# Two fused transformer blocks: both norms behind the first MLP from one inverse root, queries and keys left raw, the residual scaled when it is loaded

## The chip, the cores and the metric

The kernel runs on one core of one Trainium2 chip. The metric is the device time of one execution in microseconds (us). Engines are named as in the profile: PE is TensorE, PEld its weight loads, DVE is VectorE, ACT is ScalarE, POOL is GpSimd, SP is the SyncE queue, which here issues DMAs.

## What is computed

Two blocks run one after the other on x of 1 x 1024 x 1024 (tokens x channels). The change sits between them:

```python
# end of the first block
x = x + squared_relu_mlp(rmsnorm(x, norm_ffn), ffn_w1, ffn_w2)
x = rmsnorm(x, norm_final)            # x * rsqrt(mean(x*x) + 1e-6) * g
# start of the second block
h = rms_norm(x, norm1_g)
z = h @ w_in                          # pool, sconv, conf and attention columns
...
q = rms_norm(q, q_norm_g); k = rms_norm(k, k_norm_g)   # over 32 channels of a head half
mix = concat([y_pool, y_sconv, y_conf, y_attn])
x = x + mix @ w_out                   # residual: the normed x
h2 = rms_norm(x, norm2_g)
x = x + (silu(h2 @ w_gate) * (h2 @ w_up)) @ w_down
```

So two norms follow each other directly (norm_final, then norm1_g), and the normed x is needed twice: as input of w_in and as the residual that w_out's product is added to.

## The kernel before

**Layout.** Activations lie with channels on the 128 partitions: x is eight tiles x_k of 128 channels x 1024 tokens, 512 KB each, which live in a ring of 40 slots (`self.u`). Each matmul is done three times in split precision (high and low parts, names ending in h and l, such as hh, hl, yh, yl, wh, wl). A GEMM of one output tile is two halves of 512 tokens, each 8 x 3 matmuls into one PSUM bank, which DVE (or ACT) then evacuates.

**Order.** Generators are the tasks; `drive` (L262) runs the task with the best priority whose operands are there by the kernel's own clock model (class `Clock`, L86). The order in which the instructions come out is the order on each engine, and each engine's queue runs in order. So a different number or kind of instructions moves all that follows them.

**Norms (L1764).** When the last MLP tile is added up, DVE has two sums of squares per token: `acc` of x, `acf` of x times the gain of norm_final. `first_norms` turns them (`tokensum`, PE transposes named cs), takes the inverse root rf of the first mean (`rsqrt`, L790: 11 small dependent DVE instructions on tiles ry, rq, rp), from rf and acf the mean of the second norm, a second inverse root r1, and the product r1f. PE spreads it over partitions (`tok_bcast`, PE matmuls tb, ACT copies) as r1b, the row factor of the second block; then rf is spread as rfb.

**Residual (L1786).** `final_out` makes the residual: for each x_k ACT multiplies by the gain, POOL by rfb (tensor_tensor 128x1024), SP stores it to DRAM (xd2). At w_out (L1936) each tile is loaded again as x4 and the GEMM's halves are added to it.

**Queries and keys (L2073).** `zt` evacuates a GEMM of w_in and multiplies by r1b on DVE; only the first one (RZ = 1) is copied raw by ACT and multiplied later. `attn_qk` squares (ACT, zsq), turns (PE, zn), sums 32 channels (DVE, zv), takes an inverse root of 128x32, spreads it (PE, zb), scales, splits, and stores to DRAM (qkd), from where the attention loads it stacked (stk). Beside this POOL computes the low part wl of every weight tile.

**The rest of the second block.** In ORDER2 (L72): attention heads 0 and 1, conf (a 31-tap convolution, some 46 DVE instructions per tile), sconv, conf, sconv, attention heads 2 and 3, pool, pool. The mixed outputs y are split (yh, yl) for w_out; PE's pp matmuls are the pool's, waiting for DVE's pld.

Of the kernel before, what the change touches and what calls it, by code (L numbers as in the profile page):

```python
# [11 lines left out]
AF = mybir.ActivationFunctionType  # L12
ALU = mybir.AluOpType
# [3 lines left out]
D = 1024  # L17
# [3 lines left out]
EPS = 1e-6  # L21
# [41 lines left out]
CL = 2.5  # L63

NP = (1, 2, 3, 4, 5)

RZ = 1

W2 = 6

# [158 lines left out]
class Kern:  # L229
# [1531 lines left out]
        self.psd = self.psx.enter_context(self.tc.tile_pool(name="psd", bufs=2, space=bass.MemoryType.PSUM))  # L1761


    def first_norms(self, xs):  # L1764


        nc, gv = self.nc, self.gv
        yield [self.acc, self.acf]
        pf = yield from self.tokensum(self.acf, "vf")
        rf = yield from self.rms_col(self.acc, D)  # L1770
        v2 = self.small("v2", 8)
        nc.vector.tensor_tensor(v2, rf, rf, ALU.mult)
        nc.vector.tensor_tensor(v2, v2, pf[:, :8], ALU.mult)
        nc.vector.tensor_scalar(v2, v2, 1.0 / D, EPS, ALU.mult, ALU.add)
        r1 = yield from self.rsqrt(v2, 8)
        r1f = self.small("r1f", 8)
        nc.vector.tensor_tensor(r1f, r1, rf, ALU.mult)
        self.rb2 = self.u("r1b")
        yield from self.tok_bcast(r1f, self.rb2)
        self.ev_rb2.set(self.rb2)  # L1780
        rfb = self.u("rfb")
        yield from self.tok_bcast(rf, rfb)
        self.acc = self.acf = None
        self.spawn(self.final_out(xs, rfb), 4)

    def final_out(self, xs, rfb):  # L1786
        nc = self.nc
        for k in range(8):
            yield [rfb]
            nc.scalar.activation(xs[k], xs[k], AF.Copy, scale=self.gv[:, G_FIN + k:G_FIN + k + 1])  # L1790
            nc.gpsimd.tensor_tensor(xs[k], xs[k], rfb, ALU.mult)
            yield [xs[k]]
            nc.sync.dma_start(self.xd2[k], xs[k])
            xs[k] = None

    def bias_tiles(self):

# [47 lines left out]
    def second(self, xs, out):  # L1845

        nc = self.nc
# [13 lines left out]
        def zt(p, into=None, raw=False):  # L1861
            t = self.u(p)

            def evac(sl, ps):
                if raw:
                    nc.scalar.activation(t[:, sl], ps, AF.Copy)
                else:
                    nc.vector.tensor_tensor(t[:, sl], ps, (into or self.rb2)[:, sl], ALU.mult)
            yield from self.big(hs, evac, () if raw else extra)
            return t  # L1870
# [15 lines left out]

        self.ydirect = [k for k in self.yorder if len(ORDER2) - ND <= at[k] < len(ORDER2) and k < 4]
        self.ys, self.ev_ys, self.heads = {}, evs(6), 0
        for n, (name, j) in enumerate(ORDER2):
            if n == NL:  # L1890
                for k in self.yorder:
                    if k not in self.ydirect:
                        self.spawn(self.load_split(self.yd[k], "y", self.ys, k, self.ev_ys[k], [self.ev_y[k]]), 5)
            if name == "attn":
                for a in range(2):
                    raw = 2 * j + a < RZ
                    t = yield from zt("zqk", raw=raw)
                    self.spawn(self.attn_qk(j, a, t, raw), 1)
                t = yield from zt("zv")
                self.spawn(self.attn_v(j, t), 1)  # L1900
                for hh in range(2):
                    self.spawn(self.attention(2 * j + hh), 2)
                del t
            elif name == "conf":
                a = yield from zt("ca")
                g_ = yield from zt("cg")
                self.spawn(self.conf_in(j, a, g_), 3)
                del a, g_
            elif name == "sconv":
                c = yield from zt("sc")  # L1910
                sh = yield from zt("sh", c)
                b = yield from zt("sb")
                self.spawn(self.sconv(j, sh, b), 3)
                del c, sh, b
            else:
                z = yield from zt("zp")
                self.spawn(self.poolmix(j, z), 3)
                del z
        self.h2 = hs = None

        xs = []
        ys, ev, ev6 = self.ys, self.ev_ys, Event()
        def part(ps, w, h, n, k):
            sl = slice(h * 512, h * 512 + 512)
# [5 lines left out]
        def added(x, ps, h):  # L1930
            sl = slice(h * 512, h * 512 + 512)
            with self.tc.high_priority(PRI):
                nc.vector.tensor_tensor(x[:, sl], ps, x[:, sl], ALU.add)

        first = self.pairs_begin(38, True)
        for mt in range(8):  # L1936
            if mt > 4:
                next(first)
            if mt == 1 and ahead:
                self.wnext()  # L1940
                xs.append(x2)
                continue
            x = self.u("x4")
            nc.sync.dma_start(x, self.xd2[mt])
            xs.append(x)
            w = self.wnext()
            ahead = mt == 0 and self.heads == 4
            if ahead:

                w2 = self.wready[self.wat]  # L1950
                x2 = self.u("x4")
                nc.sync.dma_start(x2, self.xd2[1])
                d = self.s2("gm")
                ps = [self.b("gm"), self.b("gm"), d[:, 0:512], d[:, 512:1024]]
                for n, k in enumerate(self.yorder):
                    yield [ev[k]]
                    for q in range(4):
                        part(ps[q], w2 if q > 1 else w, q % 2, n, k)
                for q in range(4):
                    added(x2 if q > 1 else x, ps[q], q % 2)  # L1960
                del d, ps, w2
                continue
            for h in range(2):
                ps = self.b("gm")
                for n, k in enumerate(self.yorder):
                    yield [ev[k]]
                    part(ps, w, h, n, k)
                added(x, ps, h)
        ys.clear()
        self.spawn(self.load_split(self.yd[6], "y", ys, 6, ev6, [self.ev_y[6]]), 5)  # L1970
        yield [ev6, self.ev_o]
# [33 lines left out]
        for q in range(11):  # L2005
# [36 lines left out]
            t = self.u("ft")  # L2042
# [27 lines left out]
        for hh in range(2):  # L2070
            self.ev_vT[2 * j + hh].set(v)

    def attn_qk(self, j, a, t, raw):  # L2073
        nc, gv, cst = self.nc, self.gv, self.cst
        if raw:

            yield [t, self.ev_rb2]
            nc.vector.tensor_tensor(t, t, self.rb2, ALU.mult)
            yield [t]
        sq = self.u("zsq")  # L2080
        nc.scalar.activation(sq, t, AF.Square)
        yield [sq, self.free_s()]
        v = self.small("zv2", 32)
        for half in range(2):
            yield [self.free_s()]
            pt = self.transpose4(sq, half, "zn")
            nc.vector.tensor_reduce(v[:, half * 16:half * 16 + 16], pt.rearrange("p (c d) -> p c d", d=32), AX.X, ALU.add)

        if a == 0:
            nc.vector.tensor_scalar(v, v, 32 * EPS, None, ALU.add)  # L2090
        else:
            nc.vector.tensor_scalar(v, v, 1.0 / 32, EPS, ALU.mult, ALU.add)
        rs = yield from self.rsqrt(v, 32)
        gcol = G_QG if a == 0 else G_KG
        for hf in range(2):
            ps = yield from self.bcast4(rs[:, hf * 16:hf * 16 + 16], "zb", 4)
            sl = slice(hf * 512, hf * 512 + 512)
            nc.vector.scalar_tensor_tensor(t[:, sl], t[:, sl], gv[:, gcol:gcol + 1], ps, ALU.mult, ALU.mult)
        for x, half in enumerate(self.split_new(t, "zqk")):
            yield [half]  # L2100
            nc.sync.dma_start(self.qkd[j, a, x], half.bitcast(F32))
        self.nqk[j] += 1
        if self.nqk[j] == 2:
            self.ev_qk[j].set()
# [234 lines left out]
    def main(self):  # L2339
        self.plan()  # L2340
        xs = yield from self.mixer()
        nrm = yield from self.cross(xs)
        self.h2 = []
        self.xd2 = self.dram("xd2", [8, 128, 1024])
        self.ev_rb2 = Event()
        nc, gv = self.nc, self.gv
        gg = self.small("gg", 8, tag="gg", bufs=1)
        nc.vector.tensor_tensor(gg, gv[:, G_FIN:G_FIN + 8], gv[:, G_N1:G_N1 + 8], ALU.mult)

        def done(k, xs):  # L2350
            if k == 0:
                self.acc, self.acf = self.u("acc"), self.u("acf")
            self.h2.append(self.split_new(xs[k], "h", gg[:, k:k + 1]))
            self.sumsq(self.acc, xs[k], k == 0)
            self.sumsq(self.acf, xs[k], k == 0, gv[:, G_FIN + k:G_FIN + k + 1])
            if k == 7:
                self.spawn(self.first_norms(xs), 0)
        self.bias, self.ev_b = [[] for _ in range(4)], [Event() for _ in range(4)]
        yield from self.mlp(nrm, done)
        del nrm  # L2360
        yield from self.second(None, self.o["out"])
# [110 lines left out]
```

## Time and profile before

| | us |
|---|---|
| median of 3 runs (2617.35 to 2618.97) | 2618.58 |
| the profiled execution | 2613.1 |
| its span | 2611.2 |
| PE busy in it | 2499.2 |
| DVE busy | 1563.7 |
| ACT busy | 855.6 |
| POOL busy | 820.5 |

PE is busy for 96% of the span, so a gain has to come from PE's idle time or from PE's clock: the mean granted clock is 0.983 of full speed. Times in the rows are us from the span's start. A bracket in a row is the idle time of that engine before the instruction and what ended it.

### The profile page before, as it was taken

To read this page: it belongs to the slowest core of one execution; us is meant where nothing else is said; L and a number is where in the kernel's file an instruction comes from. 1 tells how busy PE (TensorE), PEld (TensorE's weight loads), DVE (VectorE), ACT (ScalarE), POOL (GpSimd) and SP (SyncE) were. 2 spreads that over 40 slices of the span, in tenths; PEclk is the share of its full clock that TensorE was granted. 3 is DMA by queue.
4 is the path that set the end of the run, shared out by engine and by line. 5 is a ranking of instruction groups with operands and counts; after the bars stand their busy time and mean duration, and the time that the engine had idled before them with its cause. 6 is when DMAs were issued, how large, how long until landed. Compare 5 with 4: busy or idle time off the path is not lost.

```text
span 2611.2 us, 30369 instructions
## 1 busy us (share of the span) xinstructions
PE 2499.2 (96%) x11880; PEld 2057.4 (79%) x11880; DVE 1563.7 (60%) x2316; ACT 855.6 (33%) x1220; POOL 820.5 (31%) x349
## 2 busy tenths in 40 slices
PE   8999999999989999999999798988989999999999
PEld 6788877888877888778888587776867888887887
DVE  7873767554457665553434857976676665664433
ACT  6422343333343333321213423434452222222210
POOL 1122121211244454322222421121245656662221
PEclk9999999999999999999999898999989999999999
DMA  3223156421132333542211232143222222236212
GB/s 130 77 77 94 63 173 207 171 89 49 65 129 82 120 105 121 227 145 99 98 57 49 97 105 57 41 145 93 85 81 73 81 89 89 65 128 235 81 49 89
DMA packets 99134, 268.25 MB, mean 103 GB/s; under 512 B 19976, under 2 KB 34480, under 8 KB 98992
## 3 DMA queue, kind: packets, MB, share of 16 engines
q1 hardware_dynamic: 78400, 192.40, 21.5%
q10 hardware_dynamic: 20592, 73.93, 8.5%
q8 instruction: 93, 1.52, 0.2%
q14 instruction: 49, 0.40, 0.1%
HBM read 196.55 MB, written 69.74 MB: 102 GB/s over the span
## 4 chain that ended last, share of the span: by engine, by line
PE 81%; DVE 11%; DMA 3%; issue 2%; ACT 2%; POOL 1%; SPq 0%; ACTq 0%; POOLq 0%; DVEq 0%
PE gm L210 46%; PE q L210 26%; DVE cy L210 1%; PE apo L210 1%; PE xs L210 1%; PE as L210 1%; PE xo L210 1%; DVE rq L210 1%; DVE ry L210 1%; DMA stk<-qkd 1%; POOL wl L210 1%; PE pk L210 1%; PE pb L210 1%; PE apt L210 1%; DVE sb L210 1%
## 5 line engine op out<-in xcount | busy, mean ns | idle before, releaser
L210 POOL TENSOR_TENSOR wl<-wr,wh 128x1024 fp32r<-128x1024 f32 (+1 forms) x137 | 339.7, 2481 | 1354.0 <-ACT wh L210 1302.2
L210 DVE TENSOR_TENSOR x<-gm,x 128x512 f32<-128x512 f32 x304 | 208.9, 688 | 346.2 <-PE gm L210 345.5
L210 ACT ACTIVATE wh<-wr 128x1024 fp32r<-128x1024 f32 (+2 forms) x147 | 153.2, 1042 | 621.7 <-PE gm L210 589.5
L210 PE MATMUL gm<-fhh,wh 128*128 128x512 f32 x864 | 337.6, 391 | 5.3 <-ACT fhh L210 4.6
L210 PE MATMUL gm<-fhl,wh 128*128 128x512 f32 x864 | 336.9, 390 | 1.0 <-DVE fhl L210 1.0
L210 PE MATMUL gm<-fhh,wl 128*128 128x512 f32 x864 | 336.6, 390 | 0.0
L210 PE MATMUL gm<-hh,wh 128*128 128x512 f32 x800 | 324.6, 406 | 11.5 <-ACT hh L210 7.3
L210 PE MATMUL gm<-hl,wh 128*128 128x512 f32 x800 | 318.3, 398 | 0.5 <-DVE hl L210 0.5
L210 PE MATMUL gm<-hh,wl 128*128 128x512 f32 x800 | 316.7, 396 | 0.0
L210 PEld LDWEIGHTS gm<-fhh,wh 128*128 128x128 f32 x864 | 162.2, 188 | 42.7 <-ACT fhh L210 5.4
L210 PEld LDWEIGHTS gm<-fhl,wh 128*128 128x128 f32 x864 | 162.3, 188 | 35.3 <-DVE fhl L210 2.2
L210 PEld LDWEIGHTS gm<-fhh,wl 128*128 128x128 f32 x864 | 162.3, 188 | 33.9
L210 PEld LDWEIGHTS gm<-hh,wh 128*128 128x128 f32 x800 | 152.9, 191 | 43.1 <-ACT hh L210 8.3
L210 PEld LDWEIGHTS gm<-hh,wl 128*128 128x128 f32 x800 | 152.7, 191 | 32.4 <-issue 0.5
L210 PEld LDWEIGHTS gm<-hl,wh 128*128 128x128 f32 x800 | 153.2, 191 | 31.4 <-DVE hl L210 1.9
L210 POOL TENSOR_TENSOR wl<-pr,wh 128x1024 fp32r<-128x1024 f32 x37 | 88.7, 2398 | 118.7 <-ACT wh L210 118.7
L210 POOL TENSOR_TENSOR wl<-sa,wh 128x1024 fp32r<-128x1024 f32 x37 | 89.1, 2409 | 107.3 <-ACT wh L210 104.3
L210 POOL TENSOR_TENSOR pl<-sb,ph 128x1024 fp32r<-128x1024 f32 x38 | 92.0, 2421 | 81.0 <-ACT ph L210 81.0
L210 PE MATMUL q<-th,wh 128*128 128x512 f32 x296 | 116.8, 395 | 0.0
L210 PE MATMUL q<-th,wl 128*128 128x512 f32 x296 | 116.3, 393 | 0.0
L210 PE MATMUL q<-tl,wh 128*128 128x512 f32 x296 | 116.2, 392 | 0.0
L210 PE MATMUL q<-th,p 128*128 128x512 f32 x304 | 103.5, 402 | 3.2 <-DVE pc L210 3.2
(461 smaller groups left out, 5233.6 us busy)
## 6 DMA issues: line engine op xcount, KB each, us to landing
fhr<-hd SPq DMA_DIRECT2D x54, 512.0 KB, 5.0
wr<-in_w_in_dram ACTq DMA_DIRECT2D x39, 512.0 KB, 3.5
xd<-x SPq DMA_DIRECT2D x32, 512.0 KB, 2.6
x<-xd SPq DMA_DIRECT2D x32, 512.0 KB, 5.4
pr<-in_ffn_w_dram SPq DMA_DIRECT2D x32, 512.0 KB, 3.6
wr<-in_ffn_w_dram ACTq DMA_DIRECT2D x32, 512.0 KB, 3.5
hd<-ft SPq DMA_DIRECT2D x27, 512.0 KB, 5.0
hd<-pc SPq DMA_DIRECT2D x27, 512.0 KB, 5.7
```

The source lines that it names most:

```text
L210: ins = f(*args, **kw)
```

## The change

The two means become v and v2 = 1e-6 v + mean(acf), and r1f is the one inverse root of v2; v's own root rf is taken after it and only kept as a small tile. All four query and key GEMMs are now copied raw by ACT, and the factor's place in their norm is a term 32e-6 times v2 added to the sum of squares. The unscaled x_k are stored as soon as they are there; rfb is spread only before the last of ORDER2's tiles; each residual tile is loaded by a task of its own and scaled by DVE (scalar_tensor_tensor 128x1024: times gain, times rfb).

```diff
@@ -63,8 +63,6 @@
-RZ = 1
...
@@ -1761,37 +1759,42 @@
-    def first_norms(self, xs):
+    def first_norms(self):
...
         yield [self.acc, self.acf]
+        v = yield from self.tokensum(self.acc, "v")
         pf = yield from self.tokensum(self.acf, "vf")
-        rf = yield from self.rms_col(self.acc, D)
-        v2 = self.small("v2", 8)
-        nc.vector.tensor_tensor(v2, rf, rf, ALU.mult)
-        nc.vector.tensor_tensor(v2, v2, pf[:, :8], ALU.mult)
-        nc.vector.tensor_scalar(v2, v2, 1.0 / D, EPS, ALU.mult, ALU.add)
-        r1 = yield from self.rsqrt(v2, 8)
-        r1f = self.small("r1f", 8)
-        nc.vector.tensor_tensor(r1f, r1, rf, ALU.mult)
+        self.rf = self.small("rf", 8, tag="rf", bufs=1)
+        self.v2 = self.small("v2", 8, tag="vrow", bufs=1)
+        nc.vector.tensor_scalar(v, v, 1.0 / D, EPS, ALU.mult, ALU.add)
+        nc.vector.tensor_scalar(pf, pf, 1.0 / D, None, ALU.mult)
+        nc.vector.scalar_tensor_tensor(self.v2, v, EPS, pf, ALU.mult, ALU.add)
+        self.ev_v2.set(self.v2)
+        r1f = yield from self.rsqrt(self.v2, 8)
         self.rb2 = self.u("r1b")
...
         self.ev_rb2.set(self.rb2)
-        rfb = self.u("rfb")
-        yield from self.tok_bcast(rf, rfb)
+        rf = yield from self.rsqrt(v, 8)
+        nc.vector.tensor_copy(self.rf, rf)
         self.acc = self.acf = None
-        self.spawn(self.final_out(xs, rfb), 4)
-    def final_out(self, xs, rfb):
-        nc = self.nc
-        for k in range(8):
-            yield [rfb]
-            nc.scalar.activation(xs[k], xs[k], AF.Copy, scale=self.gv[:, G_FIN + k:G_FIN + k + 1])
-            nc.gpsimd.tensor_tensor(xs[k], xs[k], rfb, ALU.mult)
-            yield [xs[k]]
-            nc.sync.dma_start(self.xd2[k], xs[k])
-            xs[k] = None
+    def residual(self, k, ev):
+        x = self.u("x4")
+        self.nc.sync.dma_start(x, self.xd2[k])
+        yield [x, self.ev_rfb]
+        self.nc.vector.scalar_tensor_tensor(x, x, self.gv[:, G_FIN + k:G_FIN + k + 1], self.rfb, ALU.mult, ALU.mult)
+        self.x4[k] = x
+        ev.set(x)
+    def final_row(self):
+        self.rfb = self.u("rfb")
+        yield from self.tok_bcast(self.rf, self.rfb)
+        self.ev_rfb.set(self.rfb)
     def bias_tiles(self):
@@ -1886,16 +1889,18 @@
         self.ys, self.ev_ys, self.heads = {}, evs(6), 0
+        self.ev_rfb, self.x4, ev4 = Event(), [None] * 8, evs(8)
         for n, (name, j) in enumerate(ORDER2):
+            if n == len(ORDER2) - 1:
+                self.spawn(self.final_row(), 4)
             if n == NL:
...
                 for a in range(2):
-                    raw = 2 * j + a < RZ
-                    t = yield from zt("zqk", raw=raw)
-                    self.spawn(self.attn_qk(j, a, t, raw), 1)
+                    t = yield from zt("zqk", raw=True)
+                    self.spawn(self.attn_qk(j, a, t), 1)
                 t = yield from zt("zv")
...
@@ -1918,7 +1923,9 @@
-        xs = []
+        xs = self.x4
+        for mt in range(2):
+            self.spawn(self.residual(mt, ev4[mt]), 4)
         ys, ev, ev6 = self.ys, self.ev_ys, Event()
         def part(ps, w, h, n, k):
...
@@ -1938,26 +1945,24 @@
                 self.wnext()
-                xs.append(x2)
+                self.spawn(self.residual(mt + 2, ev4[mt + 2]), 4)
                 continue
-            x = self.u("x4")
-            nc.sync.dma_start(x, self.xd2[mt])
-            xs.append(x)
+            if mt + 2 < 8:
+                self.spawn(self.residual(mt + 2, ev4[mt + 2]), 4)
             w = self.wnext()
...
                 w2 = self.wready[self.wat]
-                x2 = self.u("x4")
-                nc.sync.dma_start(x2, self.xd2[1])
                 d = self.s2("gm")
...
                         part(ps[q], w2 if q > 1 else w, q % 2, n, k)
+                yield ev4[:2]
                 for q in range(4):
-                    added(x2 if q > 1 else x, ps[q], q % 2)
+                    added(xs[q // 2], ps[q], q % 2)
                 del d, ps, w2
...
@@ -1965,7 +1970,12 @@
                     part(ps, w, h, n, k)
-                added(x, ps, h)
+                yield [ev4[mt]]
+                added(xs[mt], ps, h)
+        for e in ev4:
+            e.aps = []
+        self.rfb = self.x4 = None
+        self.ev_rfb.aps = []
         ys.clear()
...
@@ -2070,13 +2080,10 @@
-    def attn_qk(self, j, a, t, raw):
+    def attn_qk(self, j, a, t):
         nc, gv, cst = self.nc, self.gv, self.cst
-        if raw:
-            yield [t, self.ev_rb2]
-            nc.vector.tensor_tensor(t, t, self.rb2, ALU.mult)
-            yield [t]
+        yield [t]
         sq = self.u("zsq")
...
@@ -2085,11 +2092,12 @@
-        if a == 0:
-            nc.vector.tensor_scalar(v, v, 32 * EPS, None, ALU.add)
-        else:
-            nc.vector.tensor_scalar(v, v, 1.0 / 32, EPS, ALU.mult, ALU.add)
+        yield [v, self.ev_v2]
+        w = v.rearrange("p (t g) -> p t g", g=4)
+        nc.vector.scalar_tensor_tensor(w, self.v2.unsqueeze(2).broadcast_to([128, 8, 4]), 32 * EPS, w, ALU.mult, ALU.add)
+        if a:
+            nc.vector.tensor_scalar(v, v, 1.0 / 32, None, ALU.mult)
         rs = yield from self.rsqrt(v, 32)
...
@@ -2342,7 +2350,7 @@
         self.xd2 = self.dram("xd2", [8, 128, 1024])
-        self.ev_rb2 = Event()
+        self.ev_rb2, self.ev_v2 = Event(), Event()
         nc, gv = self.nc, self.gv
...
@@ -2353,8 +2361,10 @@
             self.sumsq(self.acf, xs[k], k == 0, gv[:, G_FIN + k:G_FIN + k + 1])
+            self.spawn(self.store(self.xd2[k], xs[k]), 2)
+            xs[k] = None
             if k == 7:
-                self.spawn(self.first_norms(xs), 0)
+                self.spawn(self.first_norms(), 0)
         self.bias, self.ev_b = [[] for _ in range(4)], [Event() for _ in range(4)]
...
```

Three places of the new order. First ACT at the start of the second block, before and then in the change (zqk: raw query or key, zsq: its square, zbr: the inverse root on its way to PE, rfb: the spread rf, x: residual tiles):

```order
L210 ACTIVATE rfb_10858<-tb_10859 128x512
L210 ACTIVATE rfb_10858<-tb_10865 128x512
L210 ACTIVATE zsq_10875<-zqk_10708 128x1024
L210 ACTIVATE x_8342<-x_8342,gv 128x1024
L210 ACTIVATE x_8344<-x_8344,gv 128x1024
L210 ACTIVATE x_8346<-x_8346,gv 128x1024
L210 ACTIVATE x_8350<-x_8350,gv 128x1024
L210 ACTIVATE wh_10947<-wr_10822 128x1024
L210 ACTIVATE zsq_10955<-zqk_10817 128x1024
```

```order
L208 ACTIVATE zqk_10715<-gm_10749 128x512
L208 ACTIVATE r1b_10813<-tb_10814 128x512
L208 ACTIVATE r1b_10813<-tb_10820 128x512
L208 ACTIVATE zsq_10862<-zqk_10715 128x1024
L208 DMA wr_10963<-in_w_in_dram 128x1024
L208 ACTIVATE zqk_10848<-gm_10855 128x512
L208 ACTIVATE zbr_10921<-ry_10893 128x512
L208 ACTIVATE zbr_10932<-ry_10893 128x512
L208 ACTIVATE zqkh_10940<-zqk_10715 128x1024
L208 ACTIVATE wh_10959<-wr_10853 128x1024
L208 ACTIVATE zqk_10848<-gm_10902 128x512
L208 ACTIVATE zsq_10973<-zqk_10848 128x1024
```

The four x rows are gone here (eight in all), and both halves of the second zqk are evacuated on ACT, ahead of its zsq.

Then DVE at the end of the pools (pld: the pool's last step, yl: low part of a mixed output, amx, ars, ap: attention heads 2), before and in the change:

```order
L210 SCALAR_TENSOR_TENSOR pld_13024<-pl_13020,cst,zp_12924 128x1008
L210 TENSOR_TENSOR pld_13024<-pl_13020,zp_12924 128x16
L210 RECIPROCAL ars_13062<-asm_12852 128x2
L210 TENSOR_SCALAR ars_13062<-asm_12852,nlam_10700,ars_13062 128x1
L210 SCALAR_TENSOR_TENSOR ap_13013<-ap_13013,ars_13062 128x128
L210 RECIPROCAL ars_13063<-asm_13048 128x2
L210 TENSOR_REDUCE amx_13060<-as_13135 128x2
L210 TENSOR_TENSOR yl_13065<-yr_12915,yh_13064 128x1024
L210 TENSOR_TENSOR yl_13069<-py_13031,yh_13068 128x1024
L210 TENSOR_SCALAR ars_13063<-asm_13048,nlam_10700,ars_13063 128x1
L210 TENSOR_REDUCE amx_13146<-as_13148 128x2
L210 TENSOR_TENSOR yl_13081<-yr_12950,yh_13080 128x1024
```

```order
L208 SCALAR_TENSOR_TENSOR pld_13013<-pl_13009,cst,zp_12892 128x1008
L208 TENSOR_TENSOR pld_13013<-pl_13009,zp_12892 128x16
L208 TENSOR_REDUCE amx_13039<-as_13041 128x2
L208 SCALAR_TENSOR_TENSOR x_2349_13017<-x_2349_13017,gv,rfb_12917 128x1024
L208 TENSOR_TENSOR yl_13027<-py_12988,yh_13026 128x1024
L208 SCALAR_TENSOR_TENSOR x_2350_13019<-x_2350_13019,gv,rfb_12917 128x1024
L208 RECIPROCAL ars_13054<-asm_12816 128x2
L208 SCALAR_TENSOR_TENSOR x_2351_13021<-x_2351_13021,gv,rfb_12917 128x1024
L208 TENSOR_SCALAR ars_13054<-asm_12816,nlam_10707,ars_13054 128x1
L208 RECIPROCAL ars_13055<-asm_13040 128x2
L208 SCALAR_TENSOR_TENSOR ap_12981<-ap_12981,ars_13054 128x128
L208 TENSOR_SCALAR ars_13055<-asm_13040,nlam_10707,ars_13055 128x1
```

Three of the eight scalings (the rows with rfb) stand ahead of most yl rows and of the first ap row.

Last SP's queue near the end of the second block's mixers (x: residual loads, stk: loads of attention head 3), before and in the change:

```order
L210 DMA x_2325_13003<-xd_1095_6242 128x1024
L210 DMA x_2380_13170<-xd_1095_6242 128x1024
L210 DMA stk_13273<-qkd_10706 64x1x1024 x2
L210 DMA stk_13276<-qkd_10706 64x1x1024 x2
L210 DMA stk_13279<-qkd_10706 64x1x1024 x2
L210 DMA stk_13282<-qkd_10706 64x1x1024 x2
L210 DMA x_2414_13307<-xd_1095_6242 128x1024
```

```order
L208 DMA x_2349_13017<-xd_1095_6242 128x1024
L208 DMA x_2350_13019<-xd_1095_6242 128x1024
L208 DMA x_2351_13021<-xd_1095_6242 128x1024
L208 DMA x_2398_13173<-xd_1095_6242 128x1024
L208 DMA stk_13275<-qkd_10713 64x1x1024 x2
L208 DMA stk_13278<-qkd_10713 64x1x1024 x2
L208 DMA stk_13281<-qkd_10713 64x1x1024 x2
L208 DMA stk_13284<-qkd_10713 64x1x1024 x2
L208 DMA x_2450_13361<-xd_1095_6242 128x1024
```

Two more residual loads stand ahead of the head's loads.

## Rows read from the trace of the kernel before

**Rows 1.** The page: the row of PE: busy us (share of the span) xinstructions.
```profile
PE 2499.2 (96%) x11880; PEld 2057.4 (79%) x11880; DVE 1563.7 (60%) x2316; ACT 855.6 (33%) x1220; POOL 820.5 (31%) x349
```

**Rows 2.** Stretches: start:end, length, busy time by engine, clock, DMA.
```profile
core 0: us, PE busy (x) PEld busy (x) DVE busy (x) ACT busy (x) POOL busy (x), PEclk, DMA share, GB/s
1480.00:1530.00 50.00, 36.25 (x164) 29.93 (x164) 30.13 (x38) 9.41 (x12) 20.61 (x9) 0.83 0.40 148
1530.00:1630.00 100.00, 91.07 (x427) 76.10 (x426) 70.49 (x101) 32.98 (x65) 18.96 (x7) 0.93 0.27 73
1630.00:1740.00 110.00, 99.89 (x537) 82.76 (x536) 104.01 (x188) 45.39 (x82) 23.25 (x9) 0.98 0.15 54
```

**Rows 3.** Timeline of PE, norms and first keys: start, duration, instruction, [idle before].
```profile
1458.78 1.03 PE L210 MATMUL cs<-cst,acf 128*128 128x128 f32 x8
1459.57 0.48 PE L210 MATMUL gm<-hh,wh 128*128 128x512 f32 x1
...
1470.02 1.94 PE L210 MATMUL tb<-cst,r1f 128*128 128x128 f32 x8 [3.06 <-DVE r1f L210]
...
1474.12 0.39 PE L210 MATMUL gm<-hh,wh 128*128 128x512 f32 x1
1474.35 0.40 PE L210 MATMUL gm<-hl,wh 128*128 128x512 f32 x1
...
1498.50 1.97 PE L210 MATMUL zn<-cst,zsq 128*128 128x128 f32 x8 [13.75 <-ACT zsq L210]
...
1504.10 0.42 PE L210 MATMUL gm<-hh,wh 128*128 128x512 f32 x1
```

**Rows 4.** Timeline of ACT: the second zsq.
```profile
1497.39 1.06 ACT L210 ACTIVATE zsq<-zqk 128x1024 f32<-128x1024 f32 x1 [13.81 <-DVE zqk L210]
```

**Rows 5.** Timeline of DVE: the norms' small instructions, then the keys' inverse root.
```profile
1462.26 0.17 DVE L210 TENSOR_SCALAR v<-v 128x8 f32<-128x8 f32 x1
...
1465.29 2.37 DVE L210 TENSOR_SCALAR ry<-v 128x8 int32<-128x8 int32 x1
...
1469.70 0.17 DVE L210 TENSOR_TENSOR r1f<-ry,ry 128x8 f32<-128x8 f32 x1
...
1479.66 2.33 DVE L210 TENSOR_SCALAR ry<-zv 128x32 int32<-128x32 int32 x1
...
1495.89 0.19 DVE L210 TENSOR_TENSOR rq<-rq,zv 128x32 f32<-128x32 f32 x1
...
1496.67 0.68 DVE L210 TENSOR_TENSOR zqk<-gm,r1b 128x512 f32<-128x512 f32 x1
```

**Rows 6.** Timeline of POOL in the same stretch.
```profile
1465.24 2.38 POOL L210 TENSOR_TENSOR wl<-wr,wh 128x1024 fp32r<-128x1024 f32 x1 [10.02 <-DVE v L210]
1474.82 18.70 POOL L210 TENSOR_TENSOR x<-x,rfb 128x1024 f32<-128x1024 f32 x8 [7.19 <-ACT rfb L210]
```

**Rows 7.** Timeline of DVE: two equal scalar_tensor_tensor 128x1024.
```profile
1448.80 1.28 DVE L210 SCALAR_TENSOR_TENSOR hl<-x,gg,hh 128x1024 fp32r<-128x1024 f32 x1 [0.28 <-ACT hh L210]
...
1453.04 3.27 DVE L210 SCALAR_TENSOR_TENSOR hl<-x,gg,hh 128x1024 fp32r<-128x1024 f32 x1
```

**Rows 8.** PE's waits, 1740 to 1890 us: total, times, longest.
```profile
PE pp L210 <- DVE pld L210: 5.5, 1, 5.5
PE gm L210 <- DVE yl L210: 2.6, 2, 1.8
```

**Rows 9.** Timeline of DVE, the pool's third sum and last step.
```profile
1757.68 1.21 DVE L210 TENSOR_TENSOR pl<-pl 128x1020 f32<-128x1020 f32 x1
...
1768.06 1.26 DVE L210 SCALAR_TENSOR_TENSOR pld<-pl,cst,zp 128x1008 f32<-128x1008 f32 x1
```

**Rows 10.** Timeline of SP: head 3's loads, then residual loads.
```profile
1774.29 25.19 SPq L210 DMA_DIRECT2D stk<-qkd  x8
1799.58 22.80 SPq L210 DMA_DIRECT2D x<-xd  x3
```

**Rows 11.** DMA issues, 1740 to 1880 us: count, size, us to landing.
```profile
x<-xd SPq DMA_DIRECT2D x8, 512.0 KB, 4.4
```

## The prediction, made before the run

> **What bounds the kernel now.** I read the page's engine row first: PE is busy for 2499.2 us, 96%, DVE for 60%, ACT for 33%, POOL for 31% [rows 1]. No other engine is near the span, so the change can only win where PE stands still or runs at a low clock. The second view is the table of stretches around the edited lines. In 1480 to 1530 PE is busy for 36.25 of 50 us at a granted clock of 0.83, and POOL for 20.61; in 1630 to 1740 it is DVE that is full, 104.01 of 110 us [rows 2]. The first stretch is where the two norms hand over to the first keys, the second is where the convolution and an attention head share DVE.
>
> The timeline of PE names the holes [rows 3]. There are two: 3.06 us before tb, ended by DVE's r1f, and 13.75 us before zn, ended by ACT's zsq. Followed back, zsq waited 13.81 us for DVE's zqk [rows 4]. That zqk is an evacuation of 0.68 us which stands in DVE's queue behind the keys' inverse root [rows 5]. One instruction of that root, 128x32, takes 2.33 us at 1479.66 and its like takes 0.19 us at 1495.89. In between POOL runs the eight products x<-x,rfb, 18.70 us from 1474.82 to 1493.52 [rows 6]. Small instructions that take 2.3 us are as long as one of POOL's (18.70 / 8 = 2.34): each waits for one of POOL's to end. So PE's large hole is POOL's residual scaling, seen through DVE's queue.
>
> **The change part by part.** The sum is made against the profiled execution, 2613.1 us (span 2611.2 and 1.9 around it). The median shown is 2618.58, 5.5 above it; I take the difference that comes out and add it to the median.
>
> *The first hole.* Before, two inverse roots follow each other: 27 small DVE instructions from v at 1462.26 to the end of r1f at 1469.87, one of them held for 2.37 us beside a POOL wl that began 0.05 us earlier [rows 5, 6]. After, r1f comes from one root; its 14 instructions are mixed with some of the other root's 11, which nothing waits for. Without a hold an instruction costs (7.61 - 2.2) / 26 = 0.2 us, so r1f is there 14 x 0.2 = 2.8 to 25 x 0.2 = 5.0 us after 1462.26, at 1465.1 to 1467.3. PE comes earlier too: before tb it passes 14 gm matmuls after the last cs where it passed 24, and 10 x 0.23 us (the distance of two starts in [rows 3]) is 2.3 us, so it arrives at 1464.7 in place of 1470.02 - 3.06 = 1466.96. The new wait is 0.4 to 2.6 us; I take 1.0, nearer the low end as the second root stands behind the first in the order. 3.06 - 1.0 = 2.1 us won.
>
> *The clock behind it.* From 1470.02 to 1474.12 PE issues two groups of eight small matmuls and three gm between them, 4.10 us. The cs group, before the wait, takes 0.79 us from its start to the next instruction, and gm 0.23 us at full clock: 2 x 0.79 + 3 x 0.23 = 2.3 us. The engine comes back from the hole at the lower of its levels (1.2 of 2.4 GHz), and that costs 1.8 us. With a hole of about 1 us I count it as won.
>
> *The second hole.* The eight POOL products are gone, and the second query or key is evacuated by ACT, so that neither the inverse root nor zqk is in front of zsq. Of 13.75 us I leave 1.0 for a wait at the next joint, the root on its way to PE or the first head's loads: 12.7 us won. From 1498.50 to 1504.10 PE again runs at half clock: eight small and nine gm take 5.60 us, where full clock makes 0.79 + 9 x 0.23 = 2.9: 2.7 us won. The stores of the residual go out earlier, and SP passes nothing that PE is waiting for. The other spread, of rf, is moved to the last mixer and not saved. ACT loses eight gain copies that were beside PE's work. This place together: 2.1 + 1.8 + 12.7 + 2.7 = 19.3 us.
>
> *DVE's full stretch.* The evacuations of the other three queries and keys go to ACT; of the two in 1530 to 1740 that is four halves of 0.68 us [rows 5] off a DVE that is full for 110 us [rows 2]. Bounds: nothing, if PE is not waiting for DVE there, and 4 x 0.68 = 2.8 us won; I take 1.5. The instructions are also mixed in another order over this stretch, by about one weight tile. The rows don't price that; PE has 210 - 191 = 19 us idle in it, and I allow a third, 6 us, either way.
>
> *The residual.* DVE gets eight scalar_tensor_tensor 128x1024. The nearest rows are the two hl, 1.28 us and, with POOL beside it, 3.27 us [rows 7]. Bounds: nothing, if they fall where PE has work ahead (PE waits for DVE only 5.5 us at pld and 2.6 at yl there [rows 8]), and 8 x 3.27 = 26.2 us if each stands in front of something PE waits for. Three do stand ahead of yl and of head 2's ap: 3 x 1.28 = 3.8 us. On the other side the wait for pld, whose steps took from 1757.68 to 1769.32 with other work between [rows 9], may shrink, by 5.5 us at most, since the order no longer has head 2's amx among them. I take 3.8 less nearly half of that 5.5, +1.5 us. Behind the loads SP holds head 3's stk, eight issues of 25.19 us in all [rows 10]; one more residual load ahead of them, 4.4 us to landing [rows 11], is hidden as long as those loads don't end a wait of PE's, and none does [rows 8].
>
> On such a pair a rule of the Trainium skill speaks against the change: the page "SBUF — State Buffer", section "Who interferes with whom", says that a DVE instruction with two SBUF inputs contends with a GpSimd instruction that reads SBUF, and calls the shared ports an exclusive lock. The trace agrees (3.27 against 1.28, and 2.37 beside a wl). Each of the eight scalings, whose x and rfb both lie in SBUF, could then be held by a wl; by the rule alone the eight would cost up to 8 x 2.0 = 16 us more. POOL is busy for a fifth of the time in the last two stretches of [rows 2], so by it one or two are held.
>
> Sum: -19.3 - 1.5 + 1.5 = -19.3 us, 2618.6 - 19.3 = 2599 us.
>
> **The rivals.**
>
> *Given back at the residual.* All eight scalings are held and stand in front of PE: -19.3 - 1.5 + 26.2 - 5.5 = -0.1, 2618.5 us. For it: DVE's queue is in order, and three are ahead of yl. Against: POOL's wl takes only a fifth of the time, and PE's waits for DVE there are 8.1 us in all [rows 8].
>
> *The residual is late: slower.* Before, a residual tile went straight into the addition; now the load, the scaling and the addition are a chain, and a scaling whose load has not landed stops DVE's whole queue, with the evacuations of w_out behind it. If slots come free late, so that six of the eight are issued only when needed, each costs 4.4 + 1.3 = 5.7 us [rows 7, 11]: 6 x 5.7 = 34, less 19.3: +15, 2633 us. It decides once a load is issued less than 4.4 us before its scaling is at the head of DVE's queue. For it: three residual loads were spread over 22.80 us before [rows 10], so SP waited for something there. Against: the loads are ordered two tiles ahead, and a tile of w_out is 48 matmuls x 0.23 = 11 us of PE.
>
> *The change doesn't do what it says.* The small 128x32 instructions are slow by themselves, and the hole moves to the next joint. Then only the first place's 3.9 us remain, 2615 us. Against: the same instruction is at 0.19 us two microseconds after POOL's last product [rows 5, 6].
>
> *More than I count.* The new order also shortens the idle time of 1530 to 1740 by the 6 us I allow, and the clock there (0.93 [rows 2]) comes up: some 7% of PE's 91 us, half of it 3 us. 2599 - 9 = 2590 us.
>
> **How the numbers follow.** Forecast 0.75, around 2599; more than I count 0.09; given back 0.06; late residual 0.06; not what it says 0.04. The range begins where every term is at its good end, -19.3 - 2.8 - 5.5 - 6 = -33.6, 2585 us, and ends at 2612, which is the forecast with +6 for the order and half of the 8 x 1.28 = 10.2 us of unheld scalings on the path, and a little (1.6) for the first wait at 2.6 in place of 1.0. The last three rivals lie above it. About 0.2%, 5.2 us, is what a measurement of this kernel can tell from no change. Faster than that are the forecast and the larger gain, 0.84; within it the give-back and the one without effect, 0.10; slower the late residual, 0.06.
>
> **What would show it.** Right: no x<-x,rfb on POOL; the keys' root in instructions of 0.2 us; PE's wait before zn under 1 us, and a clock near 1.00 in that stretch; a wait before tb of about 1 us; the scalings on DVE between 1.3 and 3.3 us, and the wait for pld below 5.5. It would be wrong if PE has a new wait of over 5 us ended by a scaling, by a residual load or by a stk load, or if the zn wait stays above 5 us without POOL beside it.

## The result: 36 us won, 17 more than forecast

| | before | after |
|---|---|---|
| median, us | 2617.97 (4 runs, 2616.12 to 2618.97) | 2581.56 (4 runs, 2574.68 to 2583.1) |
| the profiled execution | 2613.1 | 2583.1 |
| span | 2611.2 | 2581.4 |

The ratio of after to before is 0.9857, interval [0.9842, 0.9872]. Run again later, beside three other kernels, the changed kernel took 2579.63 us where before took 2614.81: 0.9859 [0.9846, 0.9872]. The time lies below the low end of the forecast range (2585).

The page's row of PE has moved little in busy time, as with before [rows 1]; it is the idle time that went:

```profile
PE 2494.7 (97%) x11880; PEld 2054.5 (80%) x11880; DVE 1546.2 (60%) x2318; ACT 850.1 (33%) x1218; POOL 802.3 (31%) x341
```

The stretches of after, with the columns of [rows 2]:

```profile
1480.00:1530.00 50.00, 50.00 (x239) 41.69 (x238) 15.40 (x33) 14.91 (x22) 9.62 (x4) 1.00 0.41 127
1530.00:1630.00 100.00, 96.62 (x511) 82.09 (x510) 94.66 (x151) 42.34 (x90) 19.34 (x8) 0.98 0.21 64
1630.00:1740.00 110.00, 99.36 (x492) 80.61 (x490) 90.68 (x149) 43.26 (x67) 26.68 (x12) 0.95 0.35 116
```

PE is now full in the first stretch at a granted clock of 1.00. The second one gained as well, 0.98 after 0.93 and 511 matmuls in place of 427, which the forecast had at almost nothing. The rows hold different work, since the changed kernel is some 18 us ahead by then; the table by stage below lays the same work side by side. The timeline of PE at the norms shows neither of the two holes of [rows 3], 3.06 and 13.75 us:

```profile
1468.63 1.06 PE L208 MATMUL tb<-cst,ry 128*128 128x128 f32 x8 [0.29 <-DVE ry L208]
...
1472.04 1.04 PE L208 MATMUL zn<-cst,zsq 128*128 128x128 f32 x8
...
1484.75 1.04 PE L208 MATMUL zn<-cst,zsq 128*128 128x128 f32 x8
```

The timeline of DVE has the keys' inverse root at full speed, 0.18 and 0.19 us, where [rows 5] had 2.33:

```profile
1474.23 0.18 DVE L208 TENSOR_SCALAR ry<-zv 128x32 int32<-128x32 int32 x1
...
1475.79 0.19 DVE L208 TENSOR_TENSOR rq<-rq,zv 128x32 f32<-128x32 f32 x1
```

The eight scalings of the residual, as the view of the tile rfb sums them up (duration min/median/max in ns, first and last start), took 1.27 us each; none took the 3.27 us of [rows 7]:

```profile
L208 DVE SCALAR_TENSOR_TENSOR x<-x,gv,rfb x8: 1262/1274/1277, 1742.9 to 1831.1; 128x1024 f32<-128x1024 f32 x8
```

And PE's waits (total, times, longest) of 1710 to 1860 us, about the same work as 1740 to 1890 of before, where [rows 8] had 5.5 us for pld:

```profile
PE pp L208 <- DVE pld L208: 3.9, 1, 3.9
PE gm L208 <- ACT yh L208: 1.9, 1, 1.9
PE apt L208 <- DVE ap L208: 1.7, 2, 1.3
PE as L208 <- DMA stk<-qkd: 1.7, 1, 1.7
PE gm L208 <- DVE yl L208: 0.5, 1, 0.5
```

**Where the time went, by stage.** Every kernel here has 11880 matmuls, so the start of the same-numbered matmul is a clock of progress that can be laid beside another trace's. The table gives the time between the 6900th, 7100th, 7300th, 7650th, 8150th and 9200th matmul, in us: the norms and first keys; the rest of the first GEMMs; the first conv; up to the pools; the pools, w_out and the start of the last MLP. Up to the 6900th these kernels differ by some 5 us (cost2 comes 8 later than before), and behind the 9200th by 2. Most of that is PE's granted clock, 0.992 to 0.995 up to the 6900th, where before happens to have the highest.

| kernel | norms, keys | GEMMs | first conv | to the pools | rest | sum |
|---|---|---|---|---|---|---|
| before | 61.3 | 43.3 | 80.1 | 104.2 | 250.1 | 539.0 |
| after, first profile | 39.8 | 43.6 | 68.7 | 104.6 | 249.3 | 505.9 |
| after, run again (again) | 39.8 | 43.8 | 68.3 | 103.4 | 248.7 | 504.1 |
| nox_same | 44.7 | 42.7 | 80.6 | 104.2 | 248.4 | 520.7 |
| nox_free | 44.2 | 43.6 | 70.7 | 102.5 | 252.8 | 513.8 |
| untold | 58.3 | 43.6 | 70.7 | 102.7 | 250.0 | 525.2 |
| oldres | 48.5 | 43.2 | 70.2 | 102.1 | 248.5 | 512.5 |
| raw1 | 40.1 | 43.9 | 69.3 | 104.2 | 248.8 | 506.3 |
| tworoots | 42.4 | 43.7 | 68.3 | 103.3 | 248.2 | 505.9 |
| noscale | 39.8 | 44.1 | 68.2 | 105.1 | 246.6 | 503.7 |
| cost2 | 39.8 | 43.7 | 70.0 | 96.8 | 272.0 | 522.3 |
| noconv | 59.6 | 42.7 | 65.3 | 106.9 | 246.0 | 520.5 |
| noconv2 | 39.8 | 43.8 | 63.4 | 101.1 | 248.9 | 497.0 |

The two profiles of the changed kernel differ by up to 1.2 us in a stage and 1.8 in the sum, so smaller differences mean nothing here. The change won 21.5 us at the norms, 11.4 to 11.8 around the first conv, and 0.4 to 2.2 in the last two stages. The 19.3 us of the forecast are the first of these. The second is what it lacks. Together the stages have 33.1 to 34.9 us of the 36.4 that the medians differ by; the rest has no place in the table. (The two profiled executions differ by only 30.0, as before's is faster than its median and after's slower.)

**The first conv, before and after.** PE's waits in before, 1555 to 1630 us (ap: softmax rows, which PE turns as apt; sb: DVE's evacuation of the product gm, after which PE can go on):

```profile
PE apt L210 <- DVE ap L210: 5.6, 2, 3.4
PE gm L210 <- DVE sb L210: 2.4, 1, 2.4
```

DVE in before, from the conv's first sum to the evacuation sb and the first softmax row ap:

```profile
1543.58 0.68 DVE L210 TENSOR_TENSOR csc<-cab 128x512 f32<-128x512 f32 x1
...
1571.92 0.68 DVE L210 TENSOR_TENSOR sb<-gm,r1b 128x512 f32<-128x512 f32 x1
...
1581.39 0.74 DVE L210 SCALAR_TENSOR_TENSOR ap<-ap,ars 128x128 f32<-128x128 f32 x2
```

The same three instructions in after:

```profile
1529.88 0.68 DVE L208 TENSOR_TENSOR csc<-cab 128x512 f32<-128x512 f32 x1
...
1530.99 0.35 DVE L208 SCALAR_TENSOR_TENSOR ap<-ap,ars 128x128 f32<-128x128 f32 x1
...
1552.46 0.68 DVE L208 TENSOR_TENSOR sb<-gm,r1b 128x512 f32<-128x512 f32 x1
```

In before ap comes 37.8 us behind the conv's first sum and sb 28.3 us behind it; the order of the two programs shows why: 40 and 31 instructions of the conv stand ahead of them in DVE's queue (28 and 22 lines of the timeline, where equal neighbours share one). In after it is 1 and 18 (1 and 14 lines), and 1.1 and 22.6 us. Nothing in the diff speaks of the conv or of the softmax. In the conv's stage PE is idle for 8.5 us in before at a mean granted clock of 0.91, and for 3.1 us in after at 0.98: the gain is about half wait and half clock.

### The profile page after: what moved, and what is told of

Same layout as the page of the kernel before. It is cut to its first block, busy times and chain, and to the rows that moved or that the text cites. A ratio compares the mean times of both kernels' runs of the same rounds, so it can differ in the third digit from the quotient of the medians.

```text
span 2581.4 us, 30345 instructions
## 1 busy us (share of the span) xinstructions
PE 2494.7 (97%) x11880; PEld 2054.5 (80%) x11880; DVE 1546.2 (60%) x2318; ACT 850.1 (33%) x1218; POOL 802.3 (31%) x341
## 4 chain that ended last, share of the span: by engine, by line
PE 82%; DVE 10%; DMA 2%; issue 2%; ACT 2%; POOL 1%; SPq 0%; ACTq 0%; POOLq 0%; DVEq 0%
PE gm L208 47%; PE q L208 26%; DVE cy L208 2%; PE xs L208 1%; PE apo L208 1%; PE as L208 1%; PE xo L208 1%; DVE csc L208 1%; DVE rq L208 1%; DVE amx L208 1%; PE pk L208 1%; PE pb L208 1%; POOL wl L208 1%; DMA wr<-in_xa_wkv_dram 1%; PE pX L208 0%
## 5 line engine op out<-in xcount | busy, mean ns | idle before, releaser
L208 PEld LDWEIGHTS gm<-fhh,wh 128*128 128x128 f32 x864 | 162.2, 188 | 42.7 <-ACT fhh L208 5.3
```

What stands on the lines that cost most here:

```text
L208: ins = f(*args, **kw)
```

## The experiments

Two theories stood at first. A: the planner (`drive` with its model `Clock`) puts out DVE's rows in a new order, and that makes the gain around the first conv. B: POOL's products, by putting DVE late, made that loss too.

**nox_same** takes POOL's products out and tells the planner that they are still there, so that no other engine's order moves:

```diff
-            nc.gpsimd.tensor_tensor(xs[k], xs[k], rfb, ALU.mult)
+            self.clock.note("gpsimd", "tensor_tensor", (xs[k], xs[k], rfb, ALU.mult), {})
```

> The kernel before without POOL's eight products x<-x,rfb (the residual stays unscaled by rfb); PE, DVE, ACT and SP keep the order of before, row for row. Theory A (the order makes the conv's gain): only the hole before zn goes with its slow clock, 13.75 + 2.7 = 16.5 us, so about 2601 us; the 10 us that the changed kernel wins around the first conv (before 1569 to 1612 us) are not won here, PE keeps its waits of 2.4 and 3.4 us for sb and ap. Theory B (POOL's products also make that loss, by putting DVE late): 16.5 + 10 = 26 us, about 2592 us. If the small instructions are slow by themselves: 2618 us, and the 128x32 ones still at 2.3 us.

Measured: 2597.31 us, 0.9935 [0.9923, 0.9947]. The norms' stage falls by 16.6 us to 44.7, the conv's stays: 80.6 against 80.1. The hole before the second zn is gone (PE's timeline):

```profile
1481.25 1.03 PE L210 MATMUL zn<-cst,zsq 128*128 128x128 f32 x8
1488.95 1.09 PE L210 MATMUL zn<-cst,zsq 128*128 128x128 f32 x8
```

and PE's waits around the conv stand as they were (1543 to 1618 us, the same work as 1555 to 1630 of before):

```profile
PE apt L210 <- DVE ap L210: 5.6, 2, 3.4
PE gm L210 <- DVE sb L210: 2.9, 1, 2.9
```

All of PE, DVE and ACT keep the order of before in this trace. So the products cost the 16.5 us that were expected of them, and nothing at the conv. B falls.

**nox_free** leaves the line out altogether; the planner mixes anew.

> The same without the eight products, but the planner is not told of them, so it mixes the instructions behind them anew (some 430 rows of PE's order differ). Theory A: 16.5 us from the hole, and up to 10 more around the first conv by the new order: 2592 to 2601 us, and below nox_same by what the order gives. Theory B: equal to nox_same within 3 us, about 2592.

Measured: 2589.54 us, 0.9902 [0.9889, 0.9915], 7.8 us below nox_same. The conv's stage is 70.7, ten less than in nox_same with the same work; the two stages behind it together give back 2.7.

**untold** is the fourth corner: the products are there, the planner does not know of them.

```diff
+            note = self.clock.note
+            self.clock.note = lambda *a: None
             nc.gpsimd.tensor_tensor(xs[k], xs[k], rfb, ALU.mult)
+            self.clock.note = note
```

> The kernel before with all its work, POOL's eight products among it, but the planner is not told of them: PE, DVE and ACT get the order of nox_free, row for row. Theory A (around the first conv only the order counts): the hole before zn stays (13 to 16 us and its slow clock), and PE's waits of 2.4 and 3.4 us around the first conv go: 7 to 8 us below before, the difference of nox_same and nox_free, about 2607 us on a chip where before takes 2614. Rival: the better order needs a DVE that POOL does not hold, then PE waits there all the same, and the time is that of before within 3 us.

Measured: 2604.8 us, 0.9959 [0.9947, 0.9971]; with all the work of before it is 10.0 us faster. The hole at the norms stays; it stands at zb now, since the new order has the first query's steps earlier (PE's timeline):

```profile
1497.79 1.11 PE L210 MATMUL zb<-cst,zbr 128*128 128x128 f32 x4 [13.19 <-ACT zbr L210]
```

That stage's row, 1480 to 1530 us, is still that of before, PE busy for 36.60 us:

```profile
1480.00:1530.00 50.00, 36.60 (x168) 29.94 (x167) 29.56 (x40) 11.84 (x15) 23.09 (x10) 0.86 0.57 189
```

The waits for sb and for DVE's ap are gone; of PE's waits from 1555 to 1620 us this one, for an ap of ACT, is left:

```profile
PE as L210 <- ACT ap L210: 1.1, 1, 1.1
```

On DVE ap and sb come 24.7 and 26.0 us behind the conv's first sum, ap ahead of sb now:

```profile
1543.05 0.68 DVE L210 TENSOR_TENSOR csc<-cab 128x512 f32<-128x512 f32 x1
...
1567.77 0.73 DVE L210 SCALAR_TENSOR_TENSOR ap<-ap,ars 128x128 f32<-128x128 f32 x2
1569.08 0.67 DVE L210 TENSOR_TENSOR sb<-gm,r1b 128x512 f32<-128x512 f32 x1
```

Theory A holds: products and order are two separate costs, 16.6 and about 10 us, each at its own place. At the conv the order is worth 9.9 us without the products and 9.4 with them. Over the whole they nearly add up: 16.9 and 10.0 us by the medians, 24.7 for both in nox_free.

**noconv, noconv2.** Is it the conv rows ahead of ap and sb? The taps 4 to 11 of the first conv are left out, in before (noconv) and in after (noconv2):

```diff
+                    row = (y[:, k:], x[:, :512 - k], t(k), y[:, k:], ALU.mult, ALU.add)
+                    if j == 0 and 4 <= k < 12:
+                        self.clock.note("vector", "scalar_tensor_tensor", row, {})
+                    else:
+                        nc.vector.scalar_tensor_tensor(*row)
```

> The kernel before with 24 of the first conv's 45 DVE rows left out (taps 4 to 11, so that conv's sums lack them); the planner still counts them, PE's order differs in 14 rows. Theory A': in before 22 and 28 of these rows stand ahead of sb and of the first ap in DVE's queue, and PE waits behind them (2.4, 3.4 and 2.2 us, and the clock behind each); with 24 rows = 16 us gone from the front of the queue these waits go, and the stretch around the conv (80 us in before) falls by 9 to 12 us: about 2603 us where before takes 2614. Rival: ap waits for ACT or for its own PE rows, then PE's waits for ap stay and the stretch falls by less than 3 us.

> The same 24 rows left out of the changed kernel. Theory A': there 1 and 14 rows stand ahead of ap and sb, and PE waits 2.0 us at most for them, so little is won, 0 to 4 us in the stretch of 69 us. Rival (DVE's load as such costs PE there, in any order): the same 9 to 12 us as in noconv.

Measured: noconv 2598.28 us, 0.9932 [0.9914, 0.9950], conv stage 65.3, 14.8 less; noconv2 2573.77 us, 0.9835 [0.9817, 0.9853], conv stage 63.4, 4.9 less than its 68.3. Both are a little above their bounds (12 and 4). The same 24 instructions are worth 9.9 us more in the order of before; the 4.9 are what they cost in the better order too. There PE's waits for sb and ap are gone and PE is full (noconv, its conv stage):

```profile
1540.00:1620.00 80.00, 79.49 (x407) 66.87 (x406) 52.43 (x82) 34.12 (x68) 15.67 (x7) 1.00 0.23 66
```

In before that place had PE busy for 51.97 of 60 us and a clock of 0.89:

```profile
1555.00:1615.00 60.00, 51.97 (x232) 43.42 (x231) 49.21 (x73) 16.94 (x39) 11.79 (x4) 0.89 0.23 62
```

**oldres** puts the old residual back into the changed kernel: the eight products behind the norms, nothing scaled at the load.

```diff
+        self.spawn(self.final_out(xs, rfb), 4)
...
-        yield [x, self.ev_rfb]
-        self.nc.vector.scalar_tensor_tensor(x, x, self.gv[:, G_FIN + k:G_FIN + k + 1], self.rfb, ALU.mult, ALU.mult)
+        yield [x]
```

> The changed kernel (one root, raw queries and keys) with the residual as before: ACT's gain, POOL's eight products x<-x,rfb and the stores behind the norms, nothing scaled at the load. Theory Q (the hole needs both POOL's products and the evacuation that stands behind the root in DVE's queue): raw evacuation by ACT frees zsq, the hole before zn is under 4 us, and the whole is 3 to 8 us above the changed kernel, 2585 to 2590. Rival P (POOL's products cost PE in any order of DVE): 15 to 25 us above, 2597 to 2607, with a hole of over 8 us that has only moved to zb or to the first head.

Measured: 2589.5 us, 0.9909 [0.9893, 0.9925], which is 0.50% above the changed kernel's 0.9859, some 13 us with 4 to either side; the traces have it at 6.6 to 8.4 us in the stages of the table, 8.7 at the norms alone. The hole is there in pieces (PE's waits of 1440 to 1520 us):

```profile
PE zb L208 <- ACT zbr L208: 3.2, 1, 3.2
PE zvT L208 <- DVE zv L208: 1.9, 1, 1.9
PE gm L208 <- DVE zv L208: 1.7, 1, 1.7
PE zn L208 <- ACT zsq L208: 1.1, 1, 1.1
```

So neither Q nor P in full: evacuating the second query by ACT frees zsq (1.1 us in place of 13.75), but 8.7 of the 16.6 us are lost at the next joints, three of them shown above.

**raw1** has only the first query raw, as before; it changes three places back (RZ = 1, the multiplication by r1b, the old epsilon).

> The changed kernel with only the first query raw, as before (the other queries and keys are evacuated by DVE and multiplied by r1b there). Theory Q: without POOL's products a root takes 11 x 0.2 = 2.2 us, the evacuation behind it is never late by more, so no hole over 2 us comes back: 0 to 4 us above the changed kernel, the 0 to 2.8 us of DVE's relief in the full stretch among it. Rival (the raw evacuation is what opens the hole): 10 us or more above it, with a PE wait of over 5 us before zn.

Measured: 2584.84 us, 0.9876 [0.9862, 0.9891]; by the medians 5.2 us above the changed kernel, with intervals that overlap, and in the stages 0.4 to 2.2 us above its two profiles, 0.3 at the norms. Without POOL's products the evacuation behind the root costs next to nothing. The raw queries are worth 2 us at most in the stages, no more than two profiles of one kernel differ.

**tworoots** makes the row factor from two roots in series again.

```diff
-        r1f = yield from self.rsqrt(self.v2, 8)
+        rf = yield from self.rsqrt(v, 8)
...
+        r1 = yield from self.rsqrt(w2, 8)
+        nc.vector.tensor_tensor(r1f, r1, rf, ALU.mult)
```

> The changed kernel with the row factor from two inverse roots in series, as before. By the sum of the prediction: the wait before tb comes back, about 3 us, and its slow clock, 1.8 us: 4 to 5 us above the changed kernel, all of it ahead of 1480 us. Rival (the gain there is from something else, or the later order takes it up): within 1.5 us of the changed kernel.

Measured: 2582.67 us, 0.9870 [0.9855, 0.9884]. The norms' stage is 2.6 us longer, with this wait (1440 to 1500 us):

```profile
PE tb L208 <- DVE r1f L208: 2.5, 1, 2.5
```

Neither bound was met: less than 4, more than 1.5. The wait came back; the granted clock stayed at 1.00 there (1455 to 1480 us), so the 1.8 us behind it did not.

**noscale** leaves the residual unscaled.

```diff
-        self.nc.vector.scalar_tensor_tensor(x, x, self.gv[:, G_FIN + k:G_FIN + k + 1], self.rfb, ALU.mult, ALU.mult)
+        self.clock.note("vector", "scalar_tensor_tensor", (x, x, self.gv[:, G_FIN + k:G_FIN + k + 1], self.rfb, ALU.mult, ALU.mult), {})
```

> The changed kernel without the eight scalings of the residual on DVE (the residual is left unscaled); the planner still counts them. Theory: they fall where PE has work ahead, so 0 to 2 us are won, 2580 to 2582 us. Rival (they stand in front of PE): 8 x 1.28 = 10 us or more won, 2571 us or less.

Measured: 2579.04 us, 0.9864 [0.9851, 0.9877], no different from the changed kernel's 0.9859; by the stages 0.4 to 2.2 us less. The 10.2 us of scalings are almost wholly beside PE's work.

**again** was the changed kernel beside untold, raw1 and tworoots; its time is in the first section, its stages are in the table.

> The changed kernel itself, beside the others on one chip: 0.986 of before, as in its first runs; its profile shows the same waits as the first one within 1 us.

**cost2, cost.** If order is worth 10 us, is a truer planner worth as much? One number is changed, from the norms on (cost2) or everywhere (cost):

```diff
-                dur = 0.065 + n * (0.00052 if op in ("tensor_copy", "tensor_scalar") else 0.00104)
+                dur = 0.065 + n * (0.00052 if op in ("tensor_copy", "tensor_scalar") else 0.00118)
```

> The changed kernel with one number of the planner changed from the norms on: it counts a DVE instruction of two inputs at 1.18 ns an element, not 1.04 (a conv row of 511 starts 0.67 us after the one before it in the trace, the planner thought 0.60). No work is added or taken; some 480 rows of PE's order and 370 of DVE's differ, all in the second block. Theory A (the order of conv rows against the attention's rows on DVE sets PE's waits here): the time moves by 3 to 10 us by the order alone, downward if a true cost makes the better order, 2570 to 2577 us where the changed kernel takes 2580. Rival (the order matters only where it was bad before): within 3 us.

> The same number changed for the whole program. Theory A: the second block as in cost2, and the first block moves by some us either way. Rival: within 3 us of the changed kernel.

Measured: cost2 2597.97 us, 0.9938 [0.9926, 0.9949], cost 2608.41 us, 0.9973 [0.9961, 0.9984]. The order alone moved the time by 16 to 18 us in the stages, upward, against the direction that I took. The conv stage stays (70.0), the stage behind it gains 7, and the last one, with the pools, loses 23 us. The kernel cost has 524.7 us in the stages; most of the other 10 us that it takes lie ahead of them, in the first block. PE's waits at the pools, 1720 to 1780 us in cost2:

```profile
PE as L209 <- DMA stk<-qkd: 8.3, 2, 7.3
PE pp L209 <- DVE v L209: 4.9, 1, 4.9
PE as L209 <- ACT ap L209: 4.3, 2, 3.9
```

What in the order makes these was not followed further.

## Why the prediction missed

*Second hole and its clock: right.* Predicted 12.7 + 2.7 = 15.4 us; nox_same has 16.6, and shows that POOL's products opened it. Evacuating by ACT alone, the other half of that term, would have closed about half of it (oldres). *First hole and its clock: right in size.* Predicted 3.9; the traces of before and after part by 3.5 us there, the wait is 0.29 us and not 1.0. In tworoots it is worth 2.6 us, as the 1.8 us for the clock are not always lost. The two waits of 1.0 us that I left for new joints did not come: 21.5 us in place of 19.3 for the place together.

*The order: the step that failed.* "The rows don't price that; PE has 210 - 191 = 19 us idle in it, and I allow a third, 6 us, either way." It stands in the sum at nothing; the first conv's stage fell by 11.4 us, 9.4 of which the order alone gives in untold. The rows shown did not price it, but the same trace did. PE's waits for sb and ap, 8.0 us in three places, are in it, with slow matmuls behind each of them; the order of the two programs shows what stood ahead of sb and ap and no longer does. I read the holes at the place that the diff edits, and for the rest used a lump. The rival that counted more (2590) had this place and 9 us for it, and I gave it 0.09. The order alone swings the time by 10 us down (untold) and by 16 to 18 up (cost2), so the lump of 6 was too small for either side. The range was too narrow by its own largest unknown, and that the order fell to the good side was luck.

*DVE's full stretch: not contradicted.* 1.5 us for the raw evacuations; raw1 has 0.4 to 2.2 in all, which is within the noise.

*The residual: right that it is small.* The sum had +1.5 us: 3.8 for scalings in front of PE, less 2.3 at pld. By noscale the scalings cost 0.4 to 2.2 us, within the noise, and the wait for pld fell from 5.5 to 3.9, by 1.6. The prediction took the two lines of [rows 8] for all of PE's waits there, 8.1 us for DVE. The view has four more, three of them for DVE, so it is 11.2 us:

```profile
PE as L210 <- DMA stk<-qkd: 1.8, 1, 1.8
PE yaT L210 <- DVE ao L210: 1.5, 1, 1.5
PE gm L210 <- DVE x L210: 1.4, 1, 1.4
PE apt L210 <- DVE ap L210: 0.2, 1, 0.2
```

That changes nothing in the sum. The load among them ends its wait at 1749.03, ahead of head 3's loads [rows 10], so that none of those ends a wait of PE's is still right; after has the same wait at 1.7 us, and none that a residual load ends.

The give-back rival needed the scalings held at 3.27 us; all took 1.27. One of them met a POOL wl, and it issued first, by 0.15 us. Timelines of DVE and POOL in after:

```profile
1759.54 1.28 DVE L208 SCALAR_TENSOR_TENSOR x<-x,gv,rfb 128x1024 f32<-128x1024 f32 x1
...
1759.69 2.82 POOL L208 TENSOR_TENSOR wl<-wr,wh 128x768 fp32r<-128x768 f32 x1 [18.81 <-DMA stk<-qkd]
```

In noscale the same wl has no scaling beside it (timeline of POOL):

```profile
1757.56 1.82 POOL L208 TENSOR_TENSOR wl<-wr,wh 128x768 fp32r<-128x768 f32 x1 [18.15 <-ACT wh L208]
```

The scaling kept its time, and the wl lost 1.00 of the 1.13 us that the scaling still had to run. That agrees with what the Trainium skill says in "SBUF — State Buffer", "Who interferes with whom", that the order of issue decides which of the two blocks. The extra 16 us that I worked out by that rule did not come, as only one in eight met a wl at all, and that one was ahead of it. The 2.37 us beside a wl that the prediction counts for the rule on two inputs is of an instruction with one tensor input (ry<-v [rows 5]); of its rows only the 3.27 us bears on that rule.

*The rival that the change doesn't do what it says: wrong*, by nox_same: the same 128x32 instructions take 0.18 to 0.19 us there, in the same order, with the products gone.

## What to carry to other kernels

Where a planner or pools set the order, a change has two effects: what it removes, and another order for everything behind it. Price the second from the trace too: list PE's waits behind the edited place, and for each look up in the new order how many rows now stand ahead of its releaser. To part the two on the chip, leave work out while the planner still counts it, and hide work from the planner while it is still done.

## What was not expected of the hardware

Eight POOL products of 18.7 us in all, with no operand that PE reads, cost PE 16.6 us, since small DVE instructions of 0.19 us, which PE's next operand stood behind in DVE's queue, went at POOL's pace of 2.3. And the clock behind a short wait is not the same each time. Before tb untold has the same wait as before [rows 3], with the eight matmuls behind it at full pace, 1.06 us in place of 1.94:

```profile
1473.47 1.06 PE L210 MATMUL tb<-cst,r1f 128*128 128x128 f32 x8 [3.07 <-DVE r1f L210]
```

The granted clock was 0.66 from 1470 to 1475 us in before, and 1.00 from 1460 to 1480 in untold. So the 1.8 us that the sum took for that clock are there in one trace and not in another; what decides it the runs don't show.
